# Filter stage of a two-layer flow trunk: three pieces of other work pinned behind a group's last filter products, query projections in the mix, weight splits at high priority

## The chip, the cores and the metric

The kernel runs on one core of one Trainium2 chip. The number compared is the device time of one execution in microseconds (us). TensorE (PE) multiplies, VectorE (DVE) and ScalarE (ACT) work element by element, GpSimd (POOL) does little here, and SyncE (SP) issues nearly all transfers. Each engine takes its instructions strictly in the order in which they stand; between engines only semaphores hold work back.

## The reference, cut to what matters

Two layers run over 1024 latent tokens and 256 context tokens of width 1024: a latent attention layer (layer 0) and a gated long convolution (layer 1). Two parts of it meet in the stage that is changed. The filters of the long convolution depend on no token, and layer 0 begins with the projections of its normalised input:

```python
for k, w in enumerate((w_in, w_hid[0], w_hid[1])):
    hdn = jnp.sin(freq[k] * (hdn @ w.astype(f32) + b[k]))
h = (hdn @ w_out.astype(f32)).reshape(L, HY_ORDER, 2, HY_WIDTH)
h = h * jnp.exp(-t * deltas)[:, None, None, :]
k_circ = jnp.concatenate([hf[:1] + hb[:1], hf[1:], jnp.zeros_like(hf[:1]), hb[:0:-1]], axis=0)
return jnp.fft.rfft(k_circ, axis=0)
...
cq, ckv, k_rope, gate = jnp.split(t @ w_in, splits, axis=-1)
q = (rmsnorm(cq, q_norm_g) @ w_uq).reshape(B, n, MLA_HEADS, MLA_NOPE + MLA_ROPE)
kv = (rmsnorm(ckv, kv_norm_g) @ w_ukv).reshape(B, n, MLA_HEADS, MLA_NOPE + MLA_V)
```

## The kernel before

Every fp32 product is done as three products of a high part and a low part (`mm3`, L115 to L121): the matmuls of L119, L120 and L121 always come as a triple. `split` (L95 to L97) makes such a pair: ACT rounds the high part (L96), DVE subtracts it (L97).

**The stage.** `layer0_in` covers the first 437 us of the span; after it the attention begins (first matmuls of `keys`). Two streams of work are interleaved there.

- *The filters* (`filters`, L284 to L362) go through eight groups of 128 channels, called group 0 to group 7 here. A group has four *filter products* (L320, L321, tile `ph`, eight matmuls of 256 columns each). DVE multiplies each by the decay (L324, `kk`) and makes sum and difference (L332, `kp`, `km`); `ph` and `kk` have one buffer each. After the fourth product comes the *ring* (`ring`, L222 and L225, tiles `rg`, `rt`, `blk`), a chain of DVE instructions that ends in eight blocks. Each block is split (`bh` on ACT, `bl` on DVE), transformed by nine matmuls on PE (tile `u`; the fifth block of a ring has twelve) and copied out by ACT (L344, `ko`), which SP stores (`kd`). A generator yields after each filter product twice and after each block once, 16 yields per group.
- *The other work* (`work`, L607) is a second generator: gate projections (`gates`), the latent's key/value projections with their norm (`latent_kv`), the context's (`context`, L534: its modulation on DVE and ACT at L425 to L427, then three projections of 256 columns, then a norm) and the adaLN matrices (`ada`, tile `ad`, four matmuls for each 512 KB pair of loads `aw`). A projection of the latent is four pieces of 12 matmuls of 512 columns (tile `pj` from `pg` and `w`). Its weights come through `weights` (L105): a load into `wr`, a split into one of three buffers `w`, one tile ahead. A norm (`rms`, `spread`) has small matmuls on PE and a row of small DVE instructions between them (L404 to L411), and a square root on ACT.

The loop at the stage's end advances the second generator by one piece for every two yields of the first. When the filters are done, `latent_q` follows: three query projections, their norm, and the last two gate projections beside it.

**What sets the order.** The framework's list scheduler takes the program as traced and places each instruction on its engine by priority and readiness; `high_priority()` lifts what is traced inside it, and `issue_after(ins)` forbids the instructions of `ins`'s engine to stand ahead of `ins`. `behind()` (L369) is `issue_after` for the last matmul that `mm3` emitted.

Of the kernel before, what the change touches and what calls it, by code (L numbers as in the profile page):

```python
# [55 lines left out]
class Net:  # L56
# [48 lines left out]
    def weights(self):  # L105

        while self.coming and len(self.loaded) < 2:
            ap = self.coming.popleft()
            n = ap.shape[-1]
            raw = self.wp.tile([P, 512], F32, tag="wr", name="wr", bufs=2)[:, :n]  # L110
            hi, lo = [self.wp.tile([P, 512], F32R, tag=f"w{r}", name="w")[:, :n] for r in range(2)]
            self.nc.sync.dma_start(out=raw, in_=ap)
            self.split(raw, hi, lo)
            self.loaded.append((hi, lo))
        return self.loaded.popleft()  # L115

# [167 lines left out]
    def filters(self, psum, pt_h, pt_u, side):  # L284
        nc, a = self.nc, self.a
# [22 lines left out]
        for g in range(KD):  # L308
            wh, wl = nxt
            kp = [gp.tile([P, 4, CS], F32, tag="rg", name=f"kp{i}") for i in range(2)]  # L310
            km = [gp.tile([P, 4, CS], F32, tag="rg", name=f"km{i}") for i in range(2)]
            for j in range(0, 8, 2):
# [3 lines left out]
                for i in range(2):  # L316
                    ts = slice(P * (j + i), P * (j + i) + P)
                    for d, h in ((0, self.hf), (1, self.hr)):
                        w = slice(256 * d, 256 * d + 256)
                        nc.tensor.matmul(ps[:, i, d], lhsT=h[:, ts], rhs=wh[:, w], start=True, stop=False)  # L320
                        nc.tensor.matmul(ps[:, i, d], lhsT=h[:, ts], rhs=wl[:, w], start=False, stop=True)  # L321
                kk = rp.tile([P, 2, 2, 2, P], F32, tag="kk", name="kk", bufs=1)
                flat = lambda t, o: t.rearrange("p i d o c -> p (i d) o c")
                nc.vector.tensor_tensor(out=flat(kk, 2), in0=flat(ps, 2), in1=flat(dec, 1).broadcast_to([P, 4, 2, P]),  # L324
# [32 lines left out]
                        nc.sync.dma_start(out=self.kd[o, g // 2, :, 2, cl], in_=kx[:, oc])  # L357

            for i, b in self.ring(two, lambda: gp.tile([P, 1024], F32, tag="rg", name="rg"), kp, km, False):
                emit(i, b)  # L360
                yield
        self.close("filtg", "filtr", "filt")  # L362


# [94 lines left out]
    def layer0_in(self):  # L459
        nc, a = self.nc, self.a  # L460
# [11 lines left out]
        self.ckv_d = [self.dram.tile([KKV, P, NK], F32, name=f"ckv_d{r}") for r in range(2)]  # L472
        self.kr_d = [self.dram.tile([65, NK], F32, name=f"kr_d{r}") for r in range(2)]
        self.silu_c()
        self.feed([a["w1"][m] for m in (0, 1, 2, 8, 9, 10, 3, 4, 8, 9, 10, 5, 11, 12, 13, 6, 7)])
        filt = self.filters(ps, "ph", "pu", "right")
        next(filt)
# [102 lines left out]
                hilo_out(t, 64, [d[0:64, sl] for d in self.kr_d])  # L580
            yield

        def latent_q():
            ts = []
            for m in (11, 12, 13):
                bs = yield from self.project(ax, bank)
                ts.append([page() for _ in halves])
                for t, b in zip(ts[-1], bs):
                    act.copy(out=t, in_=b)
                yield  # L590
            more = gates(range(6, 8))
            for h, sl in enumerate(halves):
                for _ in normed([t[h] for t in ts], "qg", self.att[3], sl, True):
                    next(more, None)
                    yield
            yield from more

        def gates(ms):
            for m in ms:
                bs = yield from self.project(ax, bank)  # L600
                for b, sl in zip(bs, halves):
                    t = st()
                    act.activation(out=t, in_=b, func=AF.Silu)
                    nc.sync.dma_start(out=self.gate_d[m, :, sl], in_=t)
                yield

        def work():  # L607
# [11 lines left out]
                yield  # L619
            for _ in gen:  # L620
                pass

        todo = work()
        n = 0
        for step, _ in enumerate(filt):
            while n * 120 < (step + 1) * 60:
                next(todo, None)
                n += 1
        for _ in todo:
# [2 lines left out]
        for c in (slice(1152, 2176), slice(0, 768), slice(768, 1152)):  # L632
            w = c.stop - c.start
# [5 lines left out]
            next(loads, None)  # L639
        for _ in loads:  # L640
            pass
        self.close("wp", "stage", "pages", "ps0")


# [807 lines left out]
```

## Time and profile before

| | |
|---|---|
| median of 3 runs | 1730.36 us (1729.24 to 1731.06) |
| the profiled execution | 1728.13 us, of which the span (first to last instruction) is 1726.3 us |
| PE busy in the span | 1625.8 us (94%) |
| DVE busy | 1437.6 us (83%) |
| ACT busy | 768.6 us (45%) |
| mean granted TensorE clock | 0.983 of full speed |
| chain that ended last | PE 78%, DMA 8%, DVE 7%, ACT 2% |

The busy times are sums over the whole span; what ends a wait is seen only in the stage itself. A matmul's busy time is longer than the distance to the next one when the two overlap, so a stretch in which PE looks busy can still run below its pace.

### The profile page before, as it was taken

How to read it: one execution, taken by the hardware profiler on the slowest of the kernel's cores; microseconds unless marked ns; L12 is line 12 of the kernel's file. 1: busy time of each engine (PE TensorE's matmuls, PEld its weight loads, DVE VectorE, ACT ScalarE, POOL GpSimd, SP SyncE). 2: the span in 40 equal slices, each digit the busy share in tenths (PEclk: the TensorE clock that was granted, in tenths of full speed). 3: DMA queues.
4: the chain of work that ended last, by engine and by line, in shares of the span. 5: the costliest groups of instructions: out<-in, count | busy, mean ns of one | idle time of the engine just before them, and what ended most of it. 6: DMA issues, size and time to landing. Idle time of an engine off the chain costs nothing.

```text
span 1726.3 us, 22764 instructions
## 1 busy us (share of the span) xinstructions
PE 1625.8 (94%) x8160; PEld 1295.0 (75%) x8160; DVE 1437.6 (83%) x2462; ACT 768.6 (45%) x1341; POOL 15.2 (1%) x43
## 2 busy tenths in 40 slices
PE   5799897899999999999999899999999999999996
PEld 1467676786788788788787677888878888887874
DVE  4886879894699899899899466999999999999956
ACT  4443444345455455555555345433433433343313
POOL 1000000000000000000000010000000000000000
PEclk8899999899999999999999999999999999999998
DMA  9877664436001011010014772332332332243545
GB/s 325 276 233 212 204 183 133 138 93 200 24 27 37 25 32 38 19 33 25 25 56 133 227 259 65 101 98 83 101 117 83 104 102 94 93 120 134 184 142 198
DMA packets 136149, 206.13 MB, mean 119 GB/s; under 512 B 13066, under 2 KB 62945, under 8 KB 135908
## 3 DMA queue, kind: packets, MB, share of 16 engines
q1 hardware_dynamic: 132900, 194.00, 35.5%
q0 software_dynamic: 3136, 10.69, 1.9%
q8 instruction: 64, 1.05, 0.3%
q14 instruction: 49, 0.40, 0.1%
HBM read 148.92 MB, written 53.61 MB: 117 GB/s over the span
## 4 chain that ended last, share of the span: by engine, by line
PE 78%; DMA 8%; DVE 7%; ACT 2%; issue 1%; SPq 1%; DVEq 0%; ACTq 0%
PE pj L121 13%; PE pj L119 13%; PE pj L120 13%; DMA aw<-in_adaw 3%; PE apx L766 2%; PE apx L767 2%; PE S L119 2%; PE O L120 2%; PE S L830 2%; PE O L119 2%; PE O L121 2%; PE S L829 2%; PE S L120 2%; PE S L121 2%; PE fu L119 2%; PE fy L119 2%
## 5 line engine op out<-in xcount | busy, mean ns | idle before, releaser
L119 PE MATMUL pj<-a,w 128*128 128x512 f32 x512 | 203.1, 397 | 1.7 <-ACT a L426 1.6
L96 ACT CAST w<-wr 128x512 fp32r<-128x512 f32 (+1 forms) x149 | 90.8, 609 | 253.5 <-PE pj L120 139.0
L120 PE MATMUL pj<-a,w 128*128 128x512 f32 x512 | 203.1, 397 | 0.0
L121 PE MATMUL pj<-a,w 128*128 128x512 f32 x512 | 203.0, 398 | 0.0
L832 ACT ACTIVATE p<-S 128x512 f32<-128x512 f32 x160 | 95.6, 597 | 148.6 <-DVE acc L839 69.5
L97 DVE TENSOR_TENSOR w<-wr,w 128x512 fp32r<-128x512 f32 (+1 forms) x149 | 98.9, 671 | 59.3 <-ACT w L96 59.2
L96 ACT CAST bh<-raw 128x512 fp32r<-128x512 f32 x128 | 77.0, 620 | 89.1 <-DVE raw L1075 71.4
L119 PEld LDWEIGHTS pj<-a,w 128*128 128x128 f32 x512 | 96.4, 188 | 22.1 <-ACT a L426 2.4
L120 PEld LDWEIGHTS pj<-a,w 128*128 128x128 f32 x512 | 96.5, 188 | 19.8 <-DVE a L427 0.3
L121 PEld LDWEIGHTS pj<-a,w 128*128 128x128 f32 x512 | 96.6, 189 | 19.4 <-issue 0.8
L97 DVE TENSOR_TENSOR p<-p 128x512 fp32r<-128x512 f32 x160 | 109.3, 684 | 1.5 <-ACT p L96 1.2
L768 DVE TENSOR_REDUCE cm<-apx 128x1 f32<-128x512 f32 (+1 forms) x192 | 107.1, 591 | 3.7 <-PE apx L767 3.1
L839 DVE TENSOR_TENSOR acc<-acc,p 128x512 f32<-128x512 f32 x144 | 98.6, 685 | 7.7 <-ACT p L832 6.7
L96 ACT CAST p<-p 128x512 fp32r<-128x512 f32 x160 | 99.5, 622 | 4.8
L121 PE MATMUL pj<-pg,w 128*128 128x512 f32 (+1 forms) x248 | 95.4, 385 | 3.5 <-DVE w L97 3.5
L119 PE MATMUL pj<-pg,w 128*128 128x512 f32 (+1 forms) x248 | 95.3, 387 | 2.2 <-ACT w L96 0.9
L120 PE MATMUL pj<-pg,w 128*128 128x512 f32 (+1 forms) x248 | 95.4, 385 | 0.0
L97 DVE TENSOR_TENSOR bl<-raw,bh 128x512 fp32r<-128x512 f32 x128 | 84.6, 685 | 9.2 <-ACT bh L96 8.9
L119 PE MATMUL u<-bh,fm 128*128 128x256 f32 (+1 forms) x200 | 67.5, 339 | 18.7 <-ACT bh L96 11.6
L766 PE MATMUL apx<-kn,qn 128*128 128x512 f32 (+1 forms) x192 | 69.1, 364 | 2.3 <-DVE cm L768 1.9
L767 PE MATMUL apx<-krh,r 128*128 128x512 f32 (+1 forms) x192 | 67.1, 357 | 0.0
L119 PE MATMUL fy<-bh,dm 128*128 128x256 f32 (+1 forms) x200 | 64.1, 321 | 2.4 <-ACT bh L96 2.4
(313 smaller groups left out, 4369.3 us busy)
## 6 DMA issues: line engine op xcount, KB each, us to landing
aw<-in_adaw SPq DMA_DIRECT2D x32, 512.0 KB, 5.0
kd<-ko SPq DMA_DIRECT2D x128, 128.0 KB, 3.3
wr<-in_hw SPq DMA_DIRECT2D x64, 256.0 KB, 3.0
kt<-kd SPq DMA_DIRECT2D x56, 256.0 KB, 2.7
wr<-in_w SPq DMA_DIRECT2D x34, 256.0 KB, 3.1
dec<-in_dec SPq DMA_DIRECT2D x32, 256.0 KB, 3.4
pg<-in_adaw SPq DMA_DIRECT2D x32, 256.0 KB, 8.0
wr<-in_wo SPq DMA_DIRECT2D x32, 256.0 KB, 3.8
```

The costliest lines, as they stand in the source:

```text
L96: self.nc.scalar.copy(out=hi, in_=raw)
L97: self.nc.vector.tensor_tensor(out=lo, in0=raw, in1=hi, op=ALU.subtract)
L119: mm(out, lhsT=w[0], rhs=x[0], start=start, stop=False)
L120: mm(out, lhsT=w[0], rhs=x[1], start=False, stop=False)
L121: self.last = mm(out, lhsT=w[1], rhs=x[0], start=False, stop=stop)
L766: mm(b[:, :w], lhsT=qn[0][:, c], rhs=kn[0][:, o : o + w], start=True, stop=False)
L767: mm(b[:, :w], lhsT=r1[:, c], rhs=krh[:, o : o + w], start=False, stop=True)
L768: v.tensor_reduce(out=cm[:, t, i : i + 1], in_=b[:, :w], axis=AX.X, op=ALU.max)
L829: mm(S, lhsT=krh[:, c], rhs=r1, start=False, stop=False)
L830: mm(S, lhsT=krl[0:65, c], rhs=r2, start=False, stop=True)
L832: act.activation(out=p, in_=S, func=AF.Exp, scale=ASCALE)
L839: v.tensor_tensor(out=acc, in0=acc, in1=p, op=ALU.add)
```

## The change

Four edits, all in the stage described above.

- In `filters`, for groups 2 to 7, the ring's first block (number 4) is no longer emitted at once: the generator first yields the group's last filter product (`end`). The loop that drives both generators then advances the other work by three pieces, with all their PE instructions queued behind that product, and the block itself is emitted behind the last `mm3` matmul.
- Beside that the other work advances by 40 pieces per 128 yields instead of 60 per 120.
- The three query projections move from `latent_q` to the end of `work` (`project_q`), so they may be advanced during the filters.
- Weight splits of the stage (`early`) are traced at high priority.

```diff
@@ -110,7 +110,8 @@
             raw = self.wp.tile([P, 512], F32, tag="wr", name="wr", bufs=2)[:, :n]
             hi, lo = [self.wp.tile([P, 512], F32R, tag=f"w{r}", name="w")[:, :n] for r in range(2)]
             self.nc.sync.dma_start(out=raw, in_=ap)
-            self.split(raw, hi, lo)
+            with self.tc.high_priority() if self.early else ExitStack():
+                self.split(raw, hi, lo)
             self.loaded.append((hi, lo))
         return self.loaded.popleft()
 
@@ -318,7 +319,7 @@
                     for d, h in ((0, self.hf), (1, self.hr)):
                         w = slice(256 * d, 256 * d + 256)
                         nc.tensor.matmul(ps[:, i, d], lhsT=h[:, ts], rhs=wh[:, w], start=True, stop=False)
-                        nc.tensor.matmul(ps[:, i, d], lhsT=h[:, ts], rhs=wl[:, w], start=False, stop=True)
+                        end = nc.tensor.matmul(ps[:, i, d], lhsT=h[:, ts], rhs=wl[:, w], start=False, stop=True)
                 kk = rp.tile([P, 2, 2, 2, P], F32, tag="kk", name="kk", bufs=1)
                 flat = lambda t, o: t.rearrange("p i d o c -> p (i d) o c")
                 nc.vector.tensor_tensor(out=flat(kk, 2), in0=flat(ps, 2), in1=flat(dec, 1).broadcast_to([P, 4, 2, P]),
@@ -357,8 +358,13 @@
                         nc.sync.dma_start(out=self.kd[o, g // 2, :, 2, cl], in_=kx[:, oc])
 
             for i, b in self.ring(two, lambda: gp.tile([P, 1024], F32, tag="rg", name="rg"), kp, km, False):
-                emit(i, b)
-                yield
+                if i == 4 and g > 1:
+                    yield end
+                    with self.behind():
+                        emit(i, b)
+                else:
+                    emit(i, b)
+                    yield
         self.close("filtg", "filtr", "filt")
 
 
@@ -472,6 +478,7 @@
         self.ckv_d = [self.dram.tile([KKV, P, NK], F32, name=f"ckv_d{r}") for r in range(2)]
         self.kr_d = [self.dram.tile([65, NK], F32, name=f"kr_d{r}") for r in range(2)]
         self.silu_c()
+        self.early = True
         self.feed([a["w1"][m] for m in (0, 1, 2, 8, 9, 10, 3, 4, 8, 9, 10, 5, 11, 12, 13, 6, 7)])
         filt = self.filters(ps, "ph", "pu", "right")
         next(filt)
@@ -580,17 +587,20 @@
                 hilo_out(t, 64, [d[0:64, sl] for d in self.kr_d])
             yield
 
-        def latent_q():
-            ts = []
+        ts_q = []
+
+        def project_q():
             for m in (11, 12, 13):
                 bs = yield from self.project(ax, bank)
-                ts.append([page() for _ in halves])
-                for t, b in zip(ts[-1], bs):
+                ts_q.append([page() for _ in halves])
+                for t, b in zip(ts_q[-1], bs):
                     act.copy(out=t, in_=b)
                 yield
+
+        def latent_q():
             more = gates(range(6, 8))
             for h, sl in enumerate(halves):
-                for _ in normed([t[h] for t in ts], "qg", self.att[3], sl, True):
+                for _ in normed([t[h] for t in ts_q], "qg", self.att[3], sl, True):
                     next(more, None)
                     yield
             yield from more
@@ -619,11 +629,16 @@
                 yield
             for _ in gen:
                 pass
+            yield from project_q()
 
         todo = work()
         n = 0
-        for step, _ in enumerate(filt):
-            while n * 120 < (step + 1) * 60:
+        for step, end in enumerate(filt):
+            if end is not None:
+                with self.tc.issue_after(end.ins):
+                    for _ in range(3):
+                        next(todo, None)
+            while n * 128 < (step + 1) * 40:
                 next(todo, None)
                 n += 1
         for _ in todo:
@@ -639,6 +654,7 @@
             next(loads, None)
         for _ in loads:
             pass
+        self.early = False
         self.close("wp", "stage", "pages", "ps0")
 
 
```

The same matmuls, DVE instructions and transfers are issued as before, and on ACT two function-table loads fewer, both at the stage's end (17 before, 15 now); their order in the stage changes. The order from the attention on is the same. Three places follow.

PE, from the last filter product of group 5 to its first ring block. Before (the rows begin with the transposes of the context's norm, `pj<-ident,st`, and the filter product is already the first of group 6):

```order
L128 MATMUL pj<-st,ones 32x256 x2
L400 MATMUL pj<-ident,st 128x64 x2
L320 MATMUL ph<-fw,hf 128x256
L321 MATMUL ph<-fw,hf 128x256
L320 MATMUL ph<-fw,hr 128x256
L321 MATMUL ph<-fw,hr 128x256
L320 MATMUL ph<-fw,hf 128x256
L321 MATMUL ph<-fw,hf 128x256
L320 MATMUL ph<-fw,hr 128x256
L321 MATMUL ph<-fw,hr 128x256
L119 MATMUL u<-bh,fm_103 128x512
L120 MATMUL u<-bl,fm_103 128x512
```

Now (the rows begin with the spread of the context's norm, `pj<-ident,rms`, which stands right behind the last filter product of group 5):

```order
L424 MATMUL pj<-ident,rms 128x128 x2
L321 MATMUL ph<-fw,hf 128x256
L322 MATMUL ph<-fw,hf 128x256
L321 MATMUL ph<-fw,hr 128x256
L322 MATMUL ph<-fw,hr 128x256
L321 MATMUL ph<-fw,hf 128x256
L322 MATMUL ph<-fw,hf 128x256
L321 MATMUL ph<-fw,hr 128x256
L322 MATMUL ph<-fw,hr 128x256
L120 MATMUL pj<-pg,w 128x256 x2
L121 MATMUL pj<-pg,w 128x256
L122 MATMUL pj<-pg,w 128x256
```

Where the first block's matmuls stood, the context's projections of 256 columns begin: 48 of them come ahead of the block.

DVE, the ring of the group beside which the context is modulated (L425 and L427 before, L431 and L433 now: 16 instructions of 128x256), up to the split `bl` of the first block. Before, in group 4:

```order
L222 SCALAR_TENSOR_TENSOR rg<-rt,km_2296 128x512
L222 SCALAR_TENSOR_TENSOR rg<-rt,km_2297 128x512
L425 SCALAR_TENSOR_TENSOR pg<-pg,gs_88,pj 128x256
L222 SCALAR_TENSOR_TENSOR rg<-rg 128x512 x2
L222 SCALAR_TENSOR_TENSOR blk<-rg 128x256 x4
L427 SCALAR_TENSOR_TENSOR pg<-pg,adac_87 128x256
L97 TENSOR_TENSOR bl<-blk,bh 128x512 x2
```

Now, in group 5:

```order
L433 SCALAR_TENSOR_TENSOR pg<-pg,adac_87 128x256
L223 SCALAR_TENSOR_TENSOR rg<-rg 128x512 x2
L223 SCALAR_TENSOR_TENSOR blk<-rg 128x256 x2
L431 SCALAR_TENSOR_TENSOR pg<-pg,gs_88,pj 128x256 x3
L433 SCALAR_TENSOR_TENSOR pg<-pg,adac_87 128x256 x3
L431 SCALAR_TENSOR_TENSOR pg<-pg,gs_88,pj 128x256 x3
L97 TENSOR_TENSOR w<-wr,w 128x512 x2
L433 SCALAR_TENSOR_TENSOR pg<-pg,adac_87 128x256 x2
L431 SCALAR_TENSOR_TENSOR pg<-pg,gs_88,pj 128x256
L433 SCALAR_TENSOR_TENSOR pg<-pg,adac_87 128x256
L97 TENSOR_TENSOR bl<-blk,bh 128x512
L433 SCALAR_TENSOR_TENSOR pg<-pg,adac_87 128x256
```

The modulation was spread over the ring's eight blocks; now 14 of its instructions and two weight splits stand between the first block's `blk` and the end of what PE needs ahead of that block.

DVE, the context's norm (L404 to L411 before, L410 to L417 now). Before, it stood among the blocks of group 5's ring. Now it stands at the head of group 6's ring, the last `kk` of the group first:

```order
L325 TENSOR_TENSOR kk<-ph,dec 128x1024
L97 TENSOR_TENSOR fw<-rt,fw 128x512
L413 RECIPROCAL rms<-rms 128x2
L333 TENSOR_TENSOR kp_3094<-kk 128x512
L414 TENSOR_TENSOR rms<-rms 128x2
L333 TENSOR_TENSOR km_3096<-kk 128x512
L415 TENSOR_TENSOR rms<-rms 128x2
L226 TENSOR_TENSOR rg<-kp_3093,kp_3094 128x1024
L416 TENSOR_SCALAR rms<-rms 128x2
L226 TENSOR_TENSOR rg<-kp_3093,kp_3094 128x1024
L417 TENSOR_TENSOR rms<-rms 128x2
```

On PE the spread of this norm (`pj<-ident,rms`, it reads the last of these rows) stands ahead of the 36 wide matmuls that are placed before group 6's first block.

## Rows read from the trace of the kernel before

**Rows 1.** Windows of core 0: the columns are named in the first line.
```profile
core 0: us, PE busy (x) PEld busy (x) DVE busy (x) ACT busy (x) POOL busy (x), PEclk, DMA share, GB/s
190.00:210.00 20.00, 13.91 (x73) 8.78 (x68) 17.16 (x37) 7.33 (x14) 0.00 (x0) 0.84 0.78 245
210.00:260.00 50.00, 47.84 (x252) 38.52 (x251) 39.07 (x68) 19.67 (x34) 0.00 (x0) 1.00 0.61 186
260.00:320.00 60.00, 43.55 (x262) 37.31 (x261) 56.10 (x111) 28.48 (x55) 0.00 (x0) 0.89 0.43 128
320.00:400.00 80.00, 78.47 (x426) 65.81 (x424) 65.81 (x112) 36.24 (x66) 2.71 (x6) 1.00 0.43 127
400.00:437.00 37.00, 33.14 (x153) 25.60 (x154) 15.51 (x34) 19.07 (x32) 0.98 (x2) 1.00 0.61 190
```

**Rows 2.** Timeline of PE (start, us, what): runs of wide and narrow matmuls.
```profile
253.63 0.39 PE L119 MATMUL pj<-pg,w 128*128 128x512 f32 x1
...
261.58 0.39 PE L121 MATMUL pj<-pg,w 128*128 128x512 f32 x1
...
287.64 0.28 PE L121 MATMUL pj<-pg,w 128*128 128x256 f32 x1
...
289.54 0.28 PE L119 MATMUL pj<-pg,w 128*128 128x256 f32 x1
```

**Rows 3.** PE groups by shape, 260 to 320 us, then 190 to 210.
```profile
L119 PE MATMUL u<-bh,fm 128*128 128x512 f32 x11 | 5.9, 553 | 10.8 <-ACT bh L96 10.8
L119 PE MATMUL pj<-pg,w 128*128 128x512 f32 x5 | 2.0, 408 | 0.0
...
L119 PE MATMUL pj<-pg,w 128*128 128x512 f32 x2 | 1.4, 702 | 0.0
```

**Rows 4.** Timeline of PE: waits in brackets, and the clock's return.
```profile
265.71 0.50 PE L119 MATMUL u<-bh,fm 128*128 128x512 f32 x1 [1.48 <-ACT bh L96]
...
280.86 0.39 PE L121 MATMUL pj<-pg,w 128*128 128x256 f32 x1 [3.53 <-DVE w L97]
...
307.89 0.80 PE L119 MATMUL u<-bh,fm 128*128 128x512 f32 x1 [8.85 <-ACT bh L96]
...
312.84 0.28 PE L119 MATMUL u<-bh,fm 128*128 128x256 f32 x1
```

**Rows 5.** Timeline of DVE and ACT: group 5's chain, last `kk` to `bh`.
```profile
296.08 1.22 DVE L324 TENSOR_TENSOR kk<-ph,dec 128x1024 f32<-128x1024 f32 x1
297.21 0.68 DVE L97 TENSOR_TENSOR fw<-rt,fw 128x512 fp32r<-128x512 f32 x1
...
299.02 2.35 DVE L225 TENSOR_TENSOR rg<-kp,kp 128x1024 f32<-128x1024 f32 x2
...
302.50 2.49 DVE L222 SCALAR_TENSOR_TENSOR rg<-rt,km 128x512 f32<-128x512 f32 x4
...
305.24 1.28 DVE L222 SCALAR_TENSOR_TENSOR rg<-rg 128x512 f32<-128x512 f32 x2
306.44 1.41 DVE L222 SCALAR_TENSOR_TENSOR blk<-rg 128x256 f32<-128x256 f32 x4
...
307.22 1.29 ACT L96 CAST bh<-blk 128x512 fp32r<-128x512 f32 x2 [7.56 <-DVE blk L222]
```

**Rows 6.** Timeline of DVE and ACT: modulation, a table load, a late weight.
```profile
273.38 1.26 DVE L425 SCALAR_TENSOR_TENSOR pg<-pg,gs,pj 128x256 f32<-128x256 f32 x3
...
308.53 1.28 ACT L406 ACT_TABLE_LOAD   x1
...
293.01 0.62 ACT L96 CAST w<-wr 128x512 fp32r<-128x512 f32 x1 [4.37 <-DMA wr<-in_w]
```

**Rows 7.** DMA issues by line, 60 to 300 us: count, KB, us to landing.
```profile
aw<-in_adaw SPq DMA_DIRECT2D x30, 512.0 KB, 5.0
```

**Rows 8.** Timeline of PE in the stage's tail.
```profile
410.63 0.50 PE L119 MATMUL pj<-pg,w 128*128 128x512 f32 x1 [0.75 <-DVE pg L527]
...
416.77 0.62 PE L418 MATMUL pj<-ident,rms 128*128 128x128 f32 x4 [1.09 <-DVE rms L411]
```

## Prediction

> **What bounds the kernel now.** I read the windows first, because the changed stage is only the first 437 us and the order behind it stays. In the stage PE is the engine that should never wait, and the windows show where it does: between 320 and 400 us it is busy 78.5 of 80 us, between 260 and 320 us only 43.6 of 60, with DVE at 56.1 and a mean granted clock of 0.89, and between 190 and 210 us 13.9 of 20 at a clock of 0.84 [rows 1]. Busy time hides part of the loss, so I turned to PE's own pace: 36 wide matmuls (512 columns) that start from 253.63 to 261.58 us are 0.227 us apart, 17 narrow ones (256 columns) from 287.64 to 289.54 us 0.119 us [rows 2]. Between 260 and 320 us there are 262 matmuls [rows 1], of which 33 wide ones of the ring (the row shown is one of three alike) and 13 wide ones of projections (5, 4 and 4) [rows 3]; 46 x 0.227 + 216 x 0.119 = 36 us of work in 60, so 24 us are lost there. From 190 to 210 us there are 5 wide ones (2, 2 and 1) among 73 [rows 1, 3]: 1.1 + 68 x 0.119 = 9.2 us, 11 us lost. Those two stretches, 35 us, are what the change can win back. The tail's 37 us hold 3.9 us of idle time, the 80 us ahead of it 1.5 us, and 210 to 260 us 2.2 us [rows 1].
>
> The waits say what ends the loss. At 307.89 us PE had waited 8.85 us for `bh`, the first block of group 5's ring; at 265.71 us 1.48 us for that of group 4; at 280.86 us 3.53 us for a weight's low part [rows 4]. The chain behind the first of these starts with the group's last `kk` at 296.08 us and runs through DVE without a gap to `bh` at 307.22 us: 11.8 us to PE's first block matmul, of which the `fw` split takes 0.6 [rows 5]. So a ring costs PE nothing if 11.8 us of other work stand behind the last filter product: 52 wide matmuls, or about 48 and a next filter product (8 x 0.119). In the order of before, groups 1 to 4 and 6 and 7 have 36 to 54 wide ones there; group 5 has none.
>
> **The change part by part.** The profiled execution took 1728.1 us (span 1726.3 us and 1.8 us around it), 2.2 us under the median of 1730.4 us. I sum against it and add the 2.2 us at the end.
>
> *Pins, groups 2, 4 and 7.* The order now has 48, 56 and 55 wide matmuls ahead of the first block. 48 x 0.227 = 10.9 us plus `ada` pieces: no wait, as before. Group 4's ring now holds three `ada` pieces within 16 us; each needs a load pair that lands 5.0 us after its issue [rows 7], and the pair's buffers come free only at the piece before, so I take 0.8, 1.2 and 0.4 us for the waits: +2.5 us (0 to 5).
>
> *Pins, group 5.* The three pieces that fall here are the context's: two hold 24 narrow matmuls, and the first is the modulation itself. Of the 16 modulations, 0.40 us each (three take 1.26 with the tail of the last) [rows 6], 14 now stand between the first block and what PE has to do ahead of it, with two weight splits of 0.6. The chain to `blk` is 11.1 us, plus 1.0 us since two splits precede the last `kk`; 14 x 0.40 + 2 x 0.6 + 0.6 for `bl` are 7.4 us, and 0.8 us lead to PE: the first block starts 20.3 us after the last filter product. PE has 48 x 0.119 + 0.95 + 0.25 = 6.9 us of work in that time. Loss 13.4 us, and 0.5 us later in the ring.
>
> *The context's norm, group 6.* The spread of this norm stands on PE ahead of the 36 pinned matmuls, and waits for DVE: `kk` 1.2, `fw`, `kp`, `km` 1.8, two `rg` of 1.13, and small ones 0.5, 5.8 us behind the last filter product; PE has 0.95 us of filter product in it. Loss 4.8 us; two filter products that now follow each other with nothing between cost 2.2 us more (one `kk` and its neighbours). The ring chain itself, 11.8 us, is then hidden by 5.8 + 36 x 0.227 = 14 us. Loss 7.0 us.
>
> *The clock.* After the 8.85 us wait the first block's wide matmul took 0.80 us, and narrow ones came down to 0.28 only at 312.84 us [rows 4]: 5 us at the slower of the two clocks, 1.2 GHz, half of them lost. The waits of groups 5 and 6 should cost that once each, less what falls into waits: 3 us (0 to 6). The Trainium skill says the same in "TensorE: Matmul & The Clock Gate", section "HAM oscillation", and more: every burst between two waits starts cold and runs at half rate. By it all 48 context matmuls of group 5 would be slow, 48 x 0.24 = 11.5 us, and the ring's start would move by some 2 us; here a narrow matmul still took 0.39 us right behind the 3.53 us wait, where the first wide one behind the 8.85 us wait took 0.80 [rows 4], so not every wait brings the slow clock, and I leave that in the range.
>
> So the stretch that lost 24 us (groups 4 to 6) loses 2.5 + 13.9 + 7.0 + 3 = 26.4 us: +2.4 us. The 8.85 us wait and the weight waits go, and the modulation, the norm and their followers are late in their place.
>
> *Group 3.* The key/value norm, which lost 11 us between 190 and 210 us, falls into the pin of group 3: its pieces are 24 wide matmuls and the norm. The chain is 11.8 us, plus 1.0 us of splits, plus a weight split inside: 13.2 us. PE has 5.5 + 0.95 + 0.5: 6.2 us lost. In the ring that follows, DVE and ACT carry the second half of the norm (20.2 us for PE's 16.4): 3.8 us. With 1.5 us for the clock 11.5 us, against 11 and the 2.2 us idle up to 260 us: -2 us (-5 to +4).
>
> *Query projections.* In the order of before 6 wide matmuls of them stood behind the last block, now 34. The 28 x 0.227 = 6.4 us only change sides. The tail's waits, 0.75 and 1.09 us among others, end with DVE on the norm [rows 8]; the two table loads that go are 1.28 us each [rows 6] on ACT, in that norm's neighbourhood. I take -1.5 us (-3 to 0).
>
> *High priority.* A weight split is 1.2 us of ACT and DVE whenever it comes; what it waits for is what costs. In the new order those of groups 3 and 4 wait for PE matmuls that are done by then, so 0. Not shown in any row: a split that blocks ACT. The nearest is 4.37 us, a split on ACT that waited for its load [rows 6]; behind it stand copies and, now, block splits. 0 to +4 us, and I take 0, since each load is issued two tiles ahead.
>
> Sum: +2.4 - 2 - 1.5 = -1.1 us, 1727.0 for the profiled execution, **1729.2 us** for the median.
>
> **The rivals.** *The long wait goes and nothing takes its place* (faster). If the context's narrow matmuls start as soon as their pieces of DVE work come, and the scheduler's order holds the modulations in DVE's free time, group 5 costs its 5 us more than the pace and group 6 its 2.2 us: 24 lost become 13, and group 3 wins 5 us by overlap: 1730 - 16 + 3 = 1717 us. For it: 8.85 us is one wait with one cause. Against it: DVE is busy 56.1 of 60 us in that stretch [rows 1], so moved work has no free time there. A milder form, with half of it, 1723 us.
>
> *The ring's chain becomes the place where everything queues* (slower). With modulations, norms and lifted weight splits all ahead of blocks on in-order engines, each of the rings of groups 3 to 6 loses 2 to 3 us more than I sum, the slow clock keeps PE at half pace through group 5's 48 narrow matmuls, and the ring ends later: +10 us, 1739 us. It decides from the point where a lifted split waits for a buffer that PE frees only after the ring's first block. For it: the 3.53 us and 4.37 us waits at weights [rows 4, 6]. Against it: three buffers, and the matmuls that free them stand ahead.
>
> *The change does nothing of what it says*: the scheduler had filled all rings but one already, and the pins replace 36 to 54 matmuls by 48 to 56 in three of six rings: 1730 us. It ends where my sum ends, and counts with it.
>
> **How the numbers follow.** About 0.2% (3.5 us) is what a measurement of this kernel can tell from no change. My sum and the third rival, 0.40, with their own range of 1726 to 1734; the faster rival and its milder form, 0.32; the slower one, 0.28. The two bounds of the terms added in quadrature give some 7 us either way; with both other cases at 8 in 10, the range is 1718 to 1740 us. Of my own case a tenth falls to each side, so: faster 0.35, within 0.2% 0.37, slower 0.28.
>
> **What would show it.** The 8.85 us wait at group 5's first block gone as one wait, and in its place some 8 us of PE waiting for the modulation and then narrow matmuls between short waits, all ahead of the block: right for that step. PE waiting about 3 us at the spread of the context's norm in group 6, and about 6 us ahead of group 3's first block: right. Two waits at `ada` loads of about 1 us in group 4's ring. A stretch from 190 us to the last block that is as long as before within 4 us, apart from the 6.4 us that move to the tail, confirms the sum. Wrong would be a group 5 that loses under 10 us, or a group 3 under 8 us (faster), or waits of ACT at weights over 3 us inside a ring (slower).

## The result, and the profile after

The changed kernel took 1744.5 us (median; 1739.1 to 1746.2) beside 1730.2 us for the kernel before: ratio 1.0082 (95% interval 1.0067 to 1.0096), 14 us slower. A second set of runs (e9 below) gave 1737.8 us beside 1727.9 us, ratio 1.0052 (1.0034 to 1.0071). The forecast was 1729.2 us, with the range ending at 1740. The first set lies beyond that end; the second lies just inside it.

The profiled execution of after took 1739.1 us (span 1737.3). Its windows, over the stretches of [rows 1] and over groups 1 and 2 (columns as there):

```profile
100.00:190.00 90.00, 85.37 (x472) 65.06 (x469) 71.81 (x122) 34.63 (x64) 0.00 (x0) 0.98 0.72 222
190.00:210.00 20.00, 14.94 (x67) 11.49 (x67) 19.19 (x39) 8.61 (x16) 0.00 (x0) 0.83 0.28 80
210.00:260.00 50.00, 47.27 (x259) 35.61 (x257) 41.92 (x76) 21.87 (x38) 0.00 (x0) 1.00 0.74 234
260.00:320.00 60.00, 46.97 (x292) 40.88 (x287) 48.96 (x90) 26.38 (x53) 0.00 (x0) 0.89 0.45 132
320.00:400.00 80.00, 74.61 (x383) 62.84 (x384) 62.84 (x113) 33.48 (x61) 2.75 (x6) 0.94 0.40 118
400.00:437.00 37.00, 30.60 (x138) 23.10 (x137) 14.21 (x32) 15.97 (x28) 0.96 (x2) 0.95 0.55 176
```

The stretch from 260 to 320 us is a little fuller than before (46.97 against 43.55 us of PE), the next 80 us are emptier (74.61 against 78.47), and the tail is emptier too (30.60 against 33.14). To add it up I count as lost, in each stretch, its length less its matmuls at full pace (wide 0.229 us and narrow 0.1185, close to the 0.227 and 0.119 of [rows 2], and 0.133 for each of the eight of an `ada` piece). These sums are estimates; another price for the small matmuls of the norms moves them by up to 1 us:

| PE lost, us | before | after | after, second profile (1731.0 us) |
|---|---|---|---|
| 100 to 190 (groups 1, 2) | 4.9 | 10.4 | 6.7 |
| 190 to 250 (group 3) | 14.8 | 11.1 | 11.3 |
| 250 to 340 (groups 4 to 6) | 24.8 | 30.6 | 28.3 |
| 340 to 400 | 2.7 | 1.5 | 1.1 |
| 400 to 440 (tail) | 4.5 | 7.9 | 10.4 |

The two profiles of after differ by 8 us, and the second is the shortest of its 7 executions (1731.0 to 1744.2). What both show: group 3 gives 3.5 us, groups 4 to 6 cost 3.5 to 6, the tail costs 3.5 to 6. In the second the stretch from 100 to 400 us as a whole stands where it stood (47.3 against 47.2 us lost); there the tail is the difference.

The attention's first matmul of `S` shows the same without any price for a matmul (before, after, second profile of after):

```profile
438.76 0.62 PE L119 MATMUL S<-qn,kn 128*128 128x512 f32 x2
448.56 0.62 PE L120 MATMUL S<-qn,kn 128*128 128x512 f32 x2
444.95 0.62 PE L120 MATMUL S<-qn,kn 128*128 128x512 f32 x2
```

The stage is 9.8 and 6.2 us longer. What follows, on PE the same matmuls in the same order, took 1284.3 to 1290.6 us in the seventeen profiles of this document, so a difference of up to 6 us between two whole executions can lie outside the stage.

What answers to the waits of [rows 4] on PE (waits in brackets; after: the first row is group 3's first block, the others lie from 250 to 345 us):

```profile
203.79 0.79 PE L120 MATMUL u<-bh,fm 128*128 128x512 f32 x1 [4.82 <-ACT bh L96]
...
259.37 1.07 PE L129 MATMUL ad<-aw,sc 128*32 128x512 f32 x8 [1.83 <-DMA aw<-in_adaw]
...
283.92 0.36 PE L321 MATMUL ph<-fw,hf 128*128 128x256 f32 x1 [2.39 <-DVE kk L325]
291.70 0.58 PE L121 MATMUL pj<-pg,w 128*128 128x256 f32 x1 [6.36 <-DVE pg L433]
294.64 0.79 PE L120 MATMUL pj<-pg,w 128*128 128x256 f32 x2 [1.71 <-ACT pg L432]
300.61 0.39 PE L121 MATMUL pj<-pg,w 128*128 128x256 f32 x1 [1.39 <-DVE pg L433]
...
323.77 0.39 PE L321 MATMUL ph<-fw,hf 128*128 128x256 f32 x1 [1.21 <-DVE kk L325]
...
326.51 0.55 PE L321 MATMUL ph<-fw,hf 128*128 128x256 f32 x1 [1.52 <-DVE kk L325]
...
328.47 0.41 PE L322 MATMUL ph<-fw,hr 128*128 128x256 f32 x1
331.04 0.69 PE L424 MATMUL pj<-ident,rms 128*128 128x128 f32 x2 [2.16 <-DVE rms L417]
331.38 0.78 PE L120 MATMUL pj<-pg,w 128*128 128x512 f32 x1
...
336.22 0.50 PE L122 MATMUL pj<-pg,w 128*128 128x512 f32 x1
```

The 8.85 us wait for group 5's first block is gone, and 11.85 us of waits for `kk` and the context's modulation stand in its place. Group 6 waits 2.16 us for the norm's spread. Behind it the projections that start from 331.38 to 336.22 us (12 of them, 11 steps) are 0.44 us apart instead of 0.229; the granted clock is 0.50 there, which is 1.2 GHz. The clock had fallen at the filter products ahead of it, between the waits of 1.52 and 2.16 us (0.41 us long there, 0.28 at full speed).

The tail, which answers to [rows 8], on PE, then ACT, then SP's queue, and last the longest of the SP queue's waits from 396 to 420 us (us in total, times, longest):

```profile
406.88 0.55 PE L406 MATMUL pj<-ident,st 96*128 96x96 f32 x4 [1.25 <-ACT st L401]
418.45 0.90 PE L406 MATMUL pj<-ident,st 96*128 96x96 f32 x4 [5.15 <-ACT st L401]
```
```profile
417.41 0.51 ACT L96 CAST wb<-pg 128x384 fp32r<-128x384 f32 x1 [6.76 <-DMA pg<-in_watt]
417.82 0.58 ACT L401 COPY st<-pj 96x512 f32<-96x512 f32 x1
```
```profile
404.40 0.43 SPq L112 DMA_DIRECT2D wr<-in_w  x1
413.20 0.34 SPq L685 DMA_DIRECT2D cos<-in_rope  x1
413.60 0.48 SPq L650 DMA_DIRECT2D pg<-in_watt  x1
```
```profile
SPq L685 <- DMA kd<-ko: 8.0, 2, 7.7
```

Read from the queue backwards: the 192 KB load for `wb` (L650) is issued at 413.60 us, behind `cos` (L685), which by the profile waits for the last filter stores `kd<-ko`. In the kernel before the same load was issued here (SP's queue of before):

```profile
322.13 0.38 SPq L635 DMA_DIRECT2D pg<-in_watt  x1
```

ACT takes its instructions in order and stands at the split of `wb` for 6.76 us. Behind it is the copy that the query norm's second column sum needs, and behind that PE. Nothing needs `wb` before the first query product of the attention, 25 us later.

### The profile page after: what moved, and what is told of

Read it like the earlier page. It is cut to its first block, busy times and chain, and to the rows that moved or that the text cites. A ratio compares the mean times of both kernels' runs of the same rounds, so it can differ in the third digit from the quotient of the medians.

```text
span 1737.3 us, 22779 instructions
## 1 busy us (share of the span) xinstructions
PE 1633.4 (94%) x8160; PEld 1299.9 (75%) x8160; DVE 1439.1 (83%) x2462; ACT 768.5 (44%) x1339; POOL 15.9 (1%) x43
## 4 chain that ended last, share of the span: by engine, by line
PE 70%; DVE 5%; DMA 3%; ACT 2%; issue 1%; SPq 0%; DVEq 0%; ACTq 0%
PE pj L120 12%; PE pj L122 12%; PE pj L121 12%; PE apx L782 2%; PE O L121 2%; PE apx L783 2%; PE S L120 2%; PE O L120 2%; PE O L122 2%; PE S L846 2%; PE S L845 2%; PE S L121 2%; PE S L122 2%; PE fu L120 2%; PE fy L120 2%; PE fy L122 2%
## 5 line engine op out<-in xcount | busy, mean ns | idle before, releaser
L120 PEld LDWEIGHTS pj<-a,w 128*128 128x128 f32 x512 | 96.4, 188 | 22.1 <-ACT a L432 2.4
L121 PE MATMUL pj<-pg,w 128*128 128x512 f32 (+1 forms) x248 | 97.6, 396 | 8.1 <-DVE pg L433 8.1
L120 PE MATMUL pj<-pg,w 128*128 128x512 f32 (+1 forms) x248 | 96.5, 396 | 1.7 <-ACT pg L432 1.7
L122 PE MATMUL pj<-pg,w 128*128 128x512 f32 (+1 forms) x248 | 97.3, 394 | 0.0
L120 PE MATMUL fu<-bh,dm 128*128 128x256 f32 (+1 forms) x200 | 64.5, 322 | 3.2 <-ACT bh L96 3.1
```

Source lines behind the costliest of these rows:

```text
L120: mm(out, lhsT=w[0], rhs=x[0], start=start, stop=False)
L121: mm(out, lhsT=w[0], rhs=x[1], start=False, stop=False)
L122: self.last = mm(out, lhsT=w[1], rhs=x[0], start=False, stop=stop)
```

## The experiments

P stands for the pins, H for the high priority, Q for the query projections in the mix. All ratios are against runs of the kernel before beside them; "tail" is PE's loss from 400 to 440 us in the profiled execution, "4 to 6" that from 250 to 340 us. "Early `wb`" and "`cq12` moved" are the two mends of the tail, told below.

| run | what is in it | ratio (interval) | 4 to 6 | tail |
|---|---|---|---|---|
| before | | 1 | 24.8 | 4.5 |
| after; e9 again | P H Q | 1.0082 (1.0067, 1.0096); 1.0052 (1.0034, 1.0071) | 30.6; 28.3 | 7.9; 10.4 |
| e1 | P H Q, cos and sin on another queue | 1.0054 (1.0042, 1.0066) | 30.3 | 7.5 |
| e2 | H Q | 0.9980 (0.9970, 0.9990) | 21.2 | 3.1 |
| e3 | P Q | 1.0050 (1.0038, 1.0062) | 27.2 | 12.5 |
| e4; e14 | H | 1.0035 (1.0023, 1.0047); 1.0023 (1.0008, 1.0038) | 26.3; 26.2 | 4.5; 6.7 |
| e5 | Q | 1.0019 (1.0007, 1.0031) | 20.7 | 10.1 |
| e6 | P H Q, early `wb` | 1.0014 (0.9999, 1.0030) | 31.2 | 1.7 |
| e7 | P | 1.0054 (1.0035, 1.0073) | 27.1 | 8.6 |
| e8 | P in 2 to 4, Q, early `wb` | 1.0053 (1.0033, 1.0072) | 20.1 | 13.1 |
| e10 | P Q, early `wb` | 0.9985 (0.9972, 0.9997) | 25.8 | 2.3 |
| e11 | e8, `cq12` moved | 1.0002 (0.9990, 1.0014) | 22.1 | 4.2 |
| e12 | H Q, early `wb`, `cq12` moved | 0.9960 (0.9948, 0.9973) | 20.7 | 2.0 |
| e13 | Q, early `wb`, `cq12` moved | 0.9971 (0.9959, 0.9984) | 20.5 | 1.4 |
| e15 | P H Q, early `wb`, `cq12` moved | 1.0004 (0.9993, 1.0016) | 32.3 | 1.3 |

**The tail's load, e1, e6 and e9.** First the queue alone:

```diff
-        nc.sync.dma_start(out=cos, in_=a["rope"][0])
-        nc.sync.dma_start(out=sin, in_=a["rope"][1])
+        nc.gpsimd.dma_start(out=cos, in_=a["rope"][0])
+        nc.gpsimd.dma_start(out=sin, in_=a["rope"][1])
```

> The changed kernel, with the loads of cos and sin moved from SP's queue to GpSimd's, so that the small load of the weights wb is no longer behind cos on SP. Theory (the tail lost 4.4 us because the second column sum's copy waited behind the split of wb, 5.15 us on TensorE): that wait goes, 4 to 6 us less than the changed kernel's 1744.5, so 1738 to 1741; the PE row at the second L406 shows a wait of about 1 us as the first does. Rival (the tail is set by the 28 query matmuls being moved and by the gates' order; the wait only takes the place of another, as the modulation's in the kernel before): 1743 to 1745, and another wait of some us stands in the tail.

The theory missed: the load was issued 8.3 us earlier, and the wait stayed (e1: SP's queue, then ACT, then PE):

```profile
404.85 0.41 SPq L692 DMA_DIRECT2D raw<-in_watt  x1
405.32 0.51 SPq L650 DMA_DIRECT2D pg<-in_watt  x1
```
```profile
416.88 0.51 ACT L96 CAST wb<-pg 128x384 fp32r<-128x384 f32 x1 [6.21 <-DMA pg<-in_watt]
```
```profile
417.92 0.90 PE L406 MATMUL pj<-ident,st 96*128 96x96 f32 x4 [4.61 <-ACT st L401]
```

It took 11.6 us from issue to split, against 3.8 us in after, and a 512 KB load (`raw`) now stands just ahead of it where in after it stood behind. The DMA engines were full at that time (e1, 396 to 430 us in 40 slices, busy share in tenths: from the fourth slice to the 21st, 399 to 414 us, all are at 9):

```profile
DMA  5689999999999999999998167993000000001607
```

So the place in the queue alone does not mend it, and the next run moves the load in time. In e6 its page is asked for ahead of the query projections:

```diff
+            wbr.append(page()[:, :384])
+            nc.sync.dma_start(out=wbr[0], in_=a["watt"][0][:, 768:1152])
             yield from project_q()
...
-        for c in (slice(1152, 2176), slice(0, 768), slice(768, 1152)):
+        for c in (slice(1152, 2176), slice(0, 768)):
...
+        raws += wbr
```

> The changed kernel, with the page for the raw weights wb asked for, and its load issued, ahead of the query projections in the mix instead of behind the mix. Moving cos and sin to another queue had left the wait at 4.61 us, since the load, though issued 8 us earlier, then took 11 us to land beside a 512 KB load issued just ahead of it. Theory (the wait is the load's landing): the wait at the second column sum's copy goes from 5.15 to about 1 us, the ratio to the kernel before falls from 1.0082 to 1.0050 to 1.0065. Rival (the tail's end is set by the chain of the gates' weights, whose last load is issued at 404 us): the wait goes, another of 3 to 5 us takes its place on TensorE between 405 and 430 us, the ratio stays 1.0075 to 1.009.

The load now leaves at 349 us. PE's waits between 396 and 440 us in e6 (engine, tile and line waited for, us in total, times, longest):

```profile
PE pj L406 <- ACT st L401: 1.0, 1, 1.0
PE pj L120 <- DVE kn L97: 0.4, 1, 0.4
```

The tail's loss falls to 1.7 us, which is 6 to 9 us less than in the two profiles of after. The ratio falls to 1.0014: 0.0038 to 0.0068 less than after, 7 to 12 us, where 3 to 5.5 us were forecast. Against the first set that is more than the 5.15 us wait of its profile, so after was profiled a second time:

> The changed kernel once more, for a second profile. Its profiled execution was the shortest of its four, 4 to 7 us below the others, and with the load of wb ahead of the projections the ratio fell by 0.0068 (12 us) where the profile had shown a wait of 5.15 us. Theory (the tail's wait for wb is longer in the usual execution, since it ends where the load lands, and the load starts where the last filter stores have landed): ratio 1.007 to 1.0095; the profile shows a wait of 8 to 12 us at the second column sum's copy if its time is near the median. Rival (the wait is 5 us in all, and the other 5 lie in the clock of groups 1 to 7): the wait is 4 to 6 us and the clock below 0.975.

```profile
414.79 0.90 PE L406 MATMUL pj<-ident,st 96*128 96x96 f32 x4 [7.29 <-ACT st L401]
```

7.29 us here, 5.15 in the first profile, 9.23 in e3: the wait ends where the load lands, and differs from one execution to the next. Neither guess is met (the ratio came to 1.0052, the wait to 7.29 us and the clock to 0.980), and this profile is of the shortest of its executions, not one near the median, so what the longest ones of after add is not seen.

**The parts apart: e2, e3, e4, e5, e7.**

```diff
-                if i == 4 and g > 1:
+                if False:
...
-            while n * 128 < (step + 1) * 40:
+            while n * 120 < (step + 1) * 58:
```

> The changed kernel without the pins (nothing is tied behind a group's last ph, pieces come at an even pace, 58 over the 120 steps), with the query projections in the mix and the high priority kept. Theory (the pins pay in group 3, 4 us, and cost in groups 4 to 6, 6 us; the losses of groups 1-2 and of the tail are not theirs): 1742 to 1745, the same as the changed kernel within 0.2%, losses of groups 1-2 and the tail's wait are still there. Rival 1 (the pins are the whole loss: they put the ring's first block late, and what follows it): 1728 to 1732. Rival 2 (the pins pay and all of the loss is elsewhere): 1750 or more.

```diff
-        self.early = True
+        self.early = False
```

> The changed kernel without the high priority of the weight splits; pins and query projections stay. Theory (the splits' place is worth nothing, as the prediction costed it; the 5.5 us of groups 1-2 come from the slower pace, which puts the loads of the modulation weights elsewhere in SP's queue): 1743 to 1746, and the two waits of TensorE for aw in 105 to 155 us are still there. Rival (the early splits take ACT and DVE from the ring's evictions and so hold the kd stores, behind which SP's loads stand): 1737 to 1740, groups 1-2 lose 5 us as in the kernel before.

e4 puts the high priority into the kernel before, e5 makes both edits above on after, e7 puts the pins and their pace into the kernel before.

> The kernel before with the high priority of the weight splits as its only change. Theory (worth nothing): 1729 to 1731.5. Rival (the early splits are what costs groups 1-2 their 5 us): 1734 to 1737 with the loss between 100 and 190 us; second rival (early splits do save the waits for w): 1726 to 1728.

> The changed kernel without pins and without the high priority: the kernel before with the query projections in the mix (58 pieces over 120 steps) as its only change. Given: without pins but with the high priority it was 0.9980 of the kernel before, the high priority alone 1.0035. Theory (the high priority costs 3 to 6 us wherever it stands, and the query projections in the mix save, because the tail then has its small load of wb early, no query matmul before its first column sum, and 28 matmuls less): 0.994 to 0.997, so 1717 to 1722 beside a before of 1727. Rival (the high priority costs only where the matmuls of the weights are few, and with 58 pieces it pays): 0.998 to 1.001.

> The kernel before with the pins alone (and the pace that goes with them): no high priority, the query projections behind the mix as before. Theory (pins gain 4 us in group 3 and 4 to 6 in group 4, cost 8 in group 5 of which they give 8 back, and cost 9 in group 6): 1.000 to 1.004. Rival 1 (pins are the whole loss of the changed kernel): 1.006 to 1.010. Rival 2 (what costs in the changed kernel is only that the query matmuls fall in groups 5 to 7, pins gain): 0.994 to 0.998.

Without pins the changed kernel beats the kernel before; my theory for e2, that the pins pay as much as they cost, is wrong, and rival 1 is nearest. The theories for e3, e4, e5 and e7 missed too. e3 came to 1.0050, which stands 0.0032 under the first set of after and 0.0002 under the second, so it cannot tell what the high priority costs. But the parts don't add: alone they cost 0.0019 to 0.0054 each, while H and Q together save 0.0020. The tails say why. In e3 it is `wb` again (9.23 us). In e7 it is a weight load that stands behind `cos` (7.81 us on ACT, 7.03 on PE). In e5 the norm's chain on DVE stands behind a split of `cq` that starts 6.12 us late (the profile gives no releaser; a split of the same kind has one in e8 below), and PE waits 6.23 us:

```profile
411.79 0.69 DVE L97 TENSOR_TENSOR cq<-pg,cq 128x512 fp32r<-128x512 f32 x1 [6.12 <-issue]
412.40 0.16 DVE L417 TENSOR_TENSOR rms<-rms 128x4 f32<-128x4 f32 x1
```

Each edit reorders ACT, DVE and SP in the tail, and which instruction then meets a load or a store that lands late (between 409 us in e7 and 421 us in e8) decides 5 to 10 us.

**The other thing that lands late: e8 and e11.** e8 keeps the pins of groups 2 to 4 (`g in (2, 3, 4)`, 49 pieces over 120 steps), with the early `wb` and no high priority.

> Pins in groups 2, 3 and 4 only (no pins where the context's modulation and its normalisation are the next pieces), the query projections in the mix, 49 pieces over 120 steps beside the 9 pinned, no high priority, and the load of wb ahead of the query projections. Theory (pins pay where the pinned pieces are plain projections, and cost where they wait for VectorE's modulation or a norm; the rest as without pins): groups 3 and 4 lose 8 to 10 us less than the kernel before, ratio 0.991 to 0.995, 1711 to 1718 beside a before of 1727. Rival (what the pins gain in groups 3 and 4 is given back by group 5, whose ring then starts from an emptier list): 0.997 to 1.000.

The theory missed: the ratio is 1.0053. DVE's longest waits between 396 and 440 us:

```profile
DVE kn L97 <- ACT kn L96: 11.4, 2, 10.7
DVE cq L97 <- DMA kd<-ko: 11.2, 1, 11.2
```

In the first DVE has nothing to do until the attention's keys come; the second is the low part of the third query tile, which by its wait lies on memory that the last filter stores read. PE waited 10.47 us behind it. e11 moves that one tile:

```diff
-        cq = [[aq.tile([P, L], F32R, name=f"cq{r}{k}") for k in range(KQ)] for r in range(2)]
+        cq = [[aq.tile([P, L], F32R, name=f"cq{r}{k}") for k in range(KQ - r)] for r in range(2)]
         cos = aq.tile([P, L], F32, name="cos")
         sin = aq.tile([P, L], F32, name="sin")
+        cq[1].append(aq.tile([P, L], F32R, name="cq12"))
```

> As e8_pins234, with the tile of the third low query part put behind cos and sin in its pool, so that it doesn't lie on memory that the last filter stores still read. In e8 VectorE waited 11.21 us for those stores at that split, and TensorE 10.47 us behind it. Theory (that one wait is what e8 lost): 8 to 10 us less, ratio 0.9990 to 1.0010. Rival (the stores' landing holds the next thing too, cos and what stands behind it, or the weights' load): 1.003 to 1.005.

1.0053 became 1.0002: 9 us, from the address of one tile. The wait for `kd<-ko` is gone from DVE. In group 3 these pins gave nothing (14.7 us lost from 190 to 250, as before): with the quicker pace the pieces of the key/value norm stand among the filter products ahead of the pin.

**What is left once the tail is mended: e10, e12, e13, e14, e15.** e12 is e2 with the two mends, e13 the same without high priority, e15 is after with the two mends, e10 is e6 without high priority. By their ratios the theories for e10, e12, e14 and e15 were met, and that for e13 was not.

> The changed kernel with the load of wb ahead of the query projections (as e6_wbuf) and without the high priority of the weight splits. Theory (the high priority costs by itself, 1.0035 on the kernel before, 1.0032 on the changed one): 0.997 to 1.000. Rival (what the high priority seemed to cost is which instruction of the tail meets a late load, and with the load mended it costs nothing): 1.000 to 1.003.

> The query projections in the mix and the high priority (as e2_nopins, 0.9980), no pins, with the load of wb ahead of the projections and the third low query part off the memory of the filter's stores. Theory (the tail of e2 lost 3.1 us to 440 us, of which some 2 are left when no load or store holds it; the rest as e2): 0.996 to 0.998. Rival (moving the load shifts the scheduler's order, and another wait stands in the tail): 0.999 to 1.002.

> As e12_mix_mended (0.9960), without the high priority of the weight splits: no pins, the query projections in the mix, both tail waits mended. Theory (the high priority costs 3 permille wherever it stands, as beside the pins: 1.0014 with, 0.9985 without): 0.992 to 0.994. Rival (it costs only where pinned pieces hold the ring's first block, since it lets splits for later weights go ahead of what the ring waits for; without pins it is worth nothing): 0.995 to 0.997. Second rival (without pins it saves the waits for w): 0.998 to 1.001.

> The kernel before with the high priority alone, once more (e4 had 1.0035, and a profiled execution below the others). Theory (it costs by itself): 1.002 to 1.005. Rival (it costs nothing, e4's runs met a slow draw): 0.999 to 1.001.

> The changed kernel, pins and high priority included, with both mends of e12 (the load of wb ahead of the query projections, the third low query part off the memory of the last filter stores). It differs from e12_mix_mended by the pins alone. Theory (the pins cost 9 us with the high priority, in groups 5 and 6): 1.000 to 1.003, groups 4 to 6 lose 28 to 32 us against 20.7 in e12. Rival (the pins cost little, and e6 with 1.0014 was held by something that the second mend takes away): 0.996 to 0.998.

The pins, with the slower pace that goes with them: e15 against e12 is 0.0044, 7.6 us. In the profiles 11.6 us are lost in groups 4 to 6 (32.3 against 20.7) and 3.4 in groups 1 and 2 (9.9 against 6.5), and 4.7 us won in group 3. PE's waits from 250 to 345 us, e15 and then e12:

```profile
PE pj L121 <- DVE pg L433: 7.7, 2, 6.2
PE ph L321 <- DVE kk L325: 5.2, 3, 2.4
PE ad L129 <- DMA aw<-in_adaw: 2.7, 2, 2.1
PE pj L424 <- DVE rms L417: 2.2, 1, 2.2
```
```profile
PE u L120 <- ACT bh L96: 9.1, 3, 7.9
PE ph L321 <- DVE kk L325: 3.4, 2, 2.2
```

With the pins the modulation and the norm are waited for; without them the ring's first block is, and it costs less. Without the high priority the pins cost less: e10 against e13 is 0.0014, and the intervals overlap (e10 has the first mend only, but none of its DVE waits in the tail is for a store). In those two profiles the stage still differs by 6.8 us (first `S` at 437.2 and 430.4 us), so how much the pins cost by themselves stays open.

The high priority: with pins 0.0029 (e6 against e10; the two intervals nearly touch, and after against e3 gives 0.0032 or 0.0002), on the kernel before 0.0035 and 0.0023, without pins and with the query projections in the mix nothing (0.9960 against 0.9971, the intervals overlap). So my theory that it costs wherever it stands fell, and the rival that ties it to the pins does not explain e4 and e14 either. What it holds up in the kernel before stays open: there `ph` waits 3.2 and 3.4 us for the norm's small steps on DVE (1.4 us in before), while the 3.53 us wait for a weight is gone.

e12 and e13 beat both kernels: 0.9960 is 7 us under the kernel before.

## Why the prediction was wrong

*Where the sum held.* The sign that I had set for it was met: from 190 to 400 us, which takes in the last block, PE loses 43.2 and 40.7 us in the two profiles of after, against 42.3 before, so the stretch is as long as before within 4 us. What failed lies ahead of that stretch and behind it.

*Group 3:* 11.5 us forecast, 11.1 and 11.3 measured, and 4.82 us of wait ahead of its first block where I had 6.2. Right.

*Groups 4 and 5:* the `ada` waits of group 4 are 0.77 and 1.83 us (forecast 0.8 and 1.2, and a third of 0.4). Group 5 has 11.85 us of waits against 13.9 us of loss forecast, for the reason given. Right in mechanism.

*Group 6 and the clock:* its waits of 1.21, 1.52 and 2.16 us are 4.9 us, where 7.0 were forecast. The stretch from 320 to 340 us lost 9.6 and 7.2 us all the same, because the clock fell a second time and stayed down to 336.4 us: the projections from 331.38 us alone lose 2.3 us. Priced by the matmuls that ran at the slower clock from 250 to 340 us, the clock cost about 6.5 and 4.9 us in the two profiles of after, an estimate, so the term of 3 us was too small. The whole stretch of groups 4 to 6 lost 3.5 to 5.8 us more than before where the sum had +2.4.

Under that term lies a misreading. I took the narrow matmul of 0.39 us behind the 3.53 us wait of before [rows 4] as the sign of a wait that cost no clock. It did cost one, later: the matmuls behind it ran at full pace up to 282.04 us, and then the clock fell (before; PE, then the window, with its columns as in [rows 1] and the clock at 0.50):

```profile
282.04 0.36 PE L121 MATMUL pj<-pg,w 128*128 128x256 f32 x1
...
283.58 0.41 PE L321 MATMUL ph<-fw,hf 128*128 128x256 f32 x1
...
285.29 0.39 PE L119 MATMUL u<-bh,fm 128*128 128x256 f32 x1
```
```profile
282.20:285.40 3.20, 3.20 (x12) 2.50 (x11) 3.20 (x6) 1.77 (x4) 0.00 (x0) 0.50 0.62 200
```

The section of the Trainium skill quoted there ("TensorE: Matmul & The Clock Gate", section "HAM oscillation") tells of a kernel whose bursts are parted by waits of about 3 to 5 us and says that each burst starts cold. Here the trace agrees behind the 6.36 us wait of after (291.70 us), where the narrow matmuls took 0.41 us from the start. The burst behind the 3.53 us wait started at full speed and turned slow within it, and in group 6 the filter products between the shorter waits of 1.52 and 2.16 us were slow, while the eight between 1.21 and 1.52 us ran at full speed.

*Groups 1 and 2*, costed at nothing: 10.4 and 6.7 us lost against 4.9. In the first profile PE waits 1.51 and 2.08 us for two loads of modulation weights, and the clock falls behind the second. The slower pace goes with it: the eight profiles that have it (after twice, e1, e3, e6, e7, e10, e15) lose 6.7 to 11.1 us there, the nine without 4.6 to 7.2. Among the nine are e8 and e11, which keep the pin of group 2, so the pin by itself does not do it; no run has the slower pace without the pins. I had followed only the pinned pieces, not the loads that the pace shifts; that the pace acts through these loads is argued: PE's waits for them grow by 1.1 us in the first profile (3.6 against 2.5), where the loss grows by 5.5.

*High priority*, costed at nothing: 5 us beside the pins, a little beyond the bound of 4 us, by the one comparison that is clear of the tail; 4 to 6 us on the kernel before, and nothing where there are no pins and the projections are in the mix.

*Query projections*, the term that stood for the tail, is the step that failed: -1.5 us forecast, +3.5 and +6 us in the profiles, and 7 to 12 us by the ratio that e6 won back. The sum looked at PE's waits in the tail of before and at the table loads. It did not ask which loads move with the projections. That of `wb` left at 322 us in the kernel before, at 386 and 391 us with the projections in the mix (e2, e5), and at 406 to 414 us with pins as well (e3, after), behind the last filter stores. So the projections alone do not put it there; and the pins alone (e7) lose 4 us more than before in the tail, at another load behind `cos`. The load takes a page, and the projections hold pages; that this is why it slid is argued, not shown. A split on ACT that waits for its load was even among the rows [rows 6], as a risk of 0 to 4 us for another part of the change. The slower rival's 1739 us was nearest in size, but its place, the rings, holds the smaller half: e6 takes 7 to 12 of the changed kernel's 9 to 14 us away with one load.

With both mends the changed kernel (e15) stands at 1.0004, where the sum had 0.9993. That is partly luck: in its profile groups 4 to 6 lose 7.5 us more than before and groups 1 and 2 lose 5 us more, which group 3 and the mended tail give back.

A slip in the chances: a tenth of 0.40 on each side makes them 0.36, 0.32 and 0.32, not 0.35, 0.37 and 0.28.

Why the longest executions of after lie 13 us above its shortest stays open. The granted clock is lower in them (0.973 at 1744.2 us against 0.980 at 1731.0 us in the second set), so more of their time lies at the slower clock, but no profile of one was taken.

## What to carry to other kernels

Where work is moved, list every load that the order moves with it, small ones and those for later stages too, and ask of each in-order queue what now stands ahead of it and who, on the engine that consumes it, stands behind. At the seam between two stages compare variants only after the late landings are out: here mending them moved five of the variants by 3 to 14 us. A pin should hold work whose inputs are ready; pinned work that waits for VectorE only moves the wait, and here it lengthened the stretches at the slower clock (250 to 340 us: 13.5 us before, 24 us after).

## What the runs showed of the hardware

A 192 KB load issued while all DMA engines were busy, behind a 512 KB one, took 11.6 us to be usable (e1), one issued 8.3 us later 3.8 us (after): both were there at about 417 us. Here, with the DMA engines full, the earlier issue alone bought 0.5 us.

Waits of 1.21 and 1.52 us, with eight narrow matmuls at full speed between them, were followed by the slower clock from 326.2 to 336.4 us (after). In the kernel before, ten narrow matmuls stood 0.12 us apart behind a wait of 3.53 us, and the clock was 0.50 from 282.1 to 285.5 us, after them. In both, matmuls at full speed stand between a wait and the fall, so the first row behind a wait does not show what the wait cost.

A tile's address decided 9 us (e8, e11): a split whose target lies on memory of the stage that had just ended waited 11.2 us until the last store from there had landed, and with the tile moved the wait was gone.
